# Placing sixteen gate tiles differently over the heads of a hybrid mLSTM and GLA layer

## The chip, the cores and the metric

The kernel runs on one core of a Trainium2 chip. The time is that of one execution on the device in microseconds (us), and the median of several runs is compared. Engines are named as the profile names them: PE does the matmuls (PEld its weight loads), DVE and ACT are the vector and the scalar engine, POOL is GpSimd, SP issues DMAs. L618 means line 618 of the kernel.

## The reference, cut to what matters

One layer works on 1024 latent tokens of width 1024 and a prefix of 256 context tokens. Its mixer projects the modulated input `u` with one wide matrix and feeds two recurrent branches, each run forwards and backwards, the context first:

```python
p = u @ w_in + b_in
q_m, k_m, v_m, o_m, g_m, q_g, k_g, v_g, z_g, r_g, gate_a, gate_b = jnp.split(p, cuts, axis=-1)
...
hm_c, hm_l = bidirectional(mlstm_scan, m_sh_c, m_g_c, m_sh_l, m_g_l, m_init)   # 8 heads of 128
hg_c, hg_l = bidirectional(gla_scan, g_sh_c, g_g_c, g_sh_l, g_g_l, g_init)     # 4 heads, keys 128, values 256
...
y_m = (head_norm(h_m, mlstm_norm_g, True) * sigmoid(o_m)) @ w_branch_mlstm
y_g = (head_norm(h_g, gla_norm_g, False) * silu(z_g)) @ w_branch_gla
mix = (sigmoid(gate_a) * y_m + sigmoid(gate_b) * y_g) @ w_out
```

A gated convolutional feed-forward block (ConvGLU) and two layer norms follow. The two pre-activations `gate_a` and `gate_b`, 1024 columns each, are needed only after both branches; they depend on nothing but `u`.

## The kernel before

**Matmuls.** Every product with a weight is made of three float32r matmuls (`mm3`, L279): high part by high part (L283), high by low (L284), low by high (L285). The high part of a weight block is copied out by ACT (L252, tile `whi`), the low part is the difference taken by DVE (L253, `wlo`); the raw block comes by a DMA on SP's queue. One projection of 128 columns by 512 tokens is 24 matmuls, each 128x128 by 128x512.

**Gate tiles.** `gate_a` and `gate_b` are computed in 16 gate tiles (`gate_tile`, L532) of 128 columns by 1024 tokens: two weight loads, two L252, two L253, 48 matmuls, two copies by ACT out of PSUM (L537), two DMAs issued by ACT (L538) to DRAM (`tha`, `thb`). `fill(n)` makes the next n of them; they are work for PE that no scan waits for. The loops over the heads say beside which head they are written down.

**Order.** The program is written in order of the loops, and the tile scheduler of the language then puts each engine's instructions into a fixed order of its own, by what is ready and by the order written. So a gate tile written behind a scan is spread into that scan's gaps on PE and behind it. The orders shown below are the scheduler's.

**GLA heads** (loop L862, h = 0 to 3). `gla_qk` and `gla_v` project, `log_gates` (L414: L423 on PE, L425, L428, L429 on ACT, L426, L430 on DVE, a DMA to `la`) makes the decay; head 0 does it for heads 1 to 3 as well. `gla_scan` (L571) loads the decay (L576) and exponentiates it (L577 on ACT), multiplies (L578), makes the diagonal (L596 on PE into the PSUM tag `pa`, L597 on DVE), and then runs seven levels, each of 16 matmuls (L618, into `pa`), two masked copies (L619, DVE), and three multiplications for either direction (L624, L626, L628; DVE, and on every second level POOL for one direction). Level l+1's L618 needs level l's L626, and L626 needs that level's L618 to have read `qq`. A tail (L639 to L692) follows. `late()` runs what a scan left over (its `finish`).

**The mLSTM's gates** (`ml_gates`, L439) run once between the two loops: a serial chain on DVE, four scans along the tokens among it (L456, L457, L461, L462). Around it lie the first v projection (`ml_proj_v(0)`; DVE copies its PSUM out at L713) and the first q and k projection (`ml_proj_qk`, L717).

**mLSTM heads** (loop L877, h = 0 to 7). Each pass projects q and k of the next head, every second pass v of the next pair, and writes down the scan of this head (`ml_scan`, L752). The scan's decay tiles come by POOL's DMA queue: L760 writes a mask, L761 adds a row to it, L764 loads another row; ACT exponentiates them (L765 once and L769 eight times for either direction), POOL multiplies (L766). PE then transposes k into the PSUM tag `pt` (L777), makes scores in `pa` (L786) and runs the state products (L796) and the outputs (L816, L817, into `po`). The transposes of the result (L844, into `pt`) and the copies of them by ACT (L845) belong to `finish`, which runs before the next scan. Tags of PSUM have two buffers each, so a third tile of tag `pt` waits until the first has been copied out.

Behind the loops come the z projection (`gated`, L918), the branch products, the output product and the feed-forward block; none of it is touched.

Of the kernel before, what the change touches and what calls it, by code (L numbers as in the profile page):

```python
# [24 lines left out]
MH = 8  # L25
# [11 lines left out]
def layer_kernel(ctx, tc, I, out, dbg=None):  # L37
# [16 lines left out]
    def nm(s):  # L54
        cnt[0] += 1
        return f"{s}_{cnt[0]}"
# [20 lines left out]
    def ubt(i, shape, dt=F32):  # L77
        return ub.tile(shape, dt, tag=f"u{i}", name=nm(f"u{i}"))
# [35 lines left out]
    for l in range(7):  # L114
        h = 1 << l
# [91 lines left out]
    for i in range(2):  # L207
        hi = stg.tile([P, 2, 256], F32R, tag="whi", name=nm("whi"), bufs=6)
        lo = stg.tile([P, 2, 256], F32R, tag="wlo", name=nm("wlo"), bufs=6)
        h, l = (t[:].rearrange("p a (b c) -> p (a b) c", c=P) for t in (hi, lo))  # L210
# [203 lines left out]
    def log_gates(h):  # L414

        for parts in (((0, 0), (0, 1)), ((1, 0), (1, 1)), ((0, 2), (1, 2))):
            t = slot(12 + zz[0] % 2, [P, SEQ])
            m = slot((14, 5)[zz[0] % 2], [P, SEQ])
            zz[0] += 1
            n = BW[parts[0][1]]  # L420
            for i, (d, b) in enumerate(parts):
                p = pt(("pa", "po", "pt")[(2 * zz[0] + i) % 3], [P, 512])
                T.matmul(p[:, 0:n], gws[d][:, h * P:(h + 1) * P], gr[0:96, b * 512:b * 512 + n], start=True, stop=True)  # L423
                bias = cB((c_gwf if d == 0 else c_gwb) + h)
                A.activation(t[:, i * n:i * n + n], p[:, 0:n], AF.Abs, bias=bias)  # L425
                V.tensor_scalar(m[:, i * n:i * n + n], p[:, 0:n], bias, 0.0, op0=ALU.add, op1=ALU.min)  # L426
            t, m = t[:, 0:2 * n], m[:, 0:2 * n]
            A.activation(t, t, AF.Exp, scale=-1.0)  # L428
            A.activation(t, t, AF.Ln, bias=ones[:])  # L429
            V.tensor_tensor(m, m, t, op=ALU.subtract)  # L430
            if n == 512:
                SY.dma_start(la_d[parts[0][0]][h][:, 0:SEQ], m)
            else:
                for d in range(2):
                    SY.dma_start(la_d[d][h][:, SEQ:L], m[:, d * n:d * n + n])
# [96 lines left out]
    def gate_tile(dst, off, cb0, j, tags=("pj", "pj")):  # L532
        w = wtile(w_in, off + j * P)
        for b in range(2):
            p = proj(w, 0, b, tags[b])
            t = sc.tile([P, 512], F32, tag="gt", name=nm("gt"), bufs=2)
            A.activation(t[:], p[:], AF.Identity, scale=0.5, bias=cB(cb0 + j))  # L537
            A.dma_start(dst[j][:, b * 512:b * 512 + 512], t[:])  # L538

    def gla_qk(h):  # L540
        w = wload([(w_in, O_QG + h * P, P, 0), (w_in, O_KG + h * P, P, P)], eng=V)
        q = slot(0, [P, SEQ])
        k = slot(1, [P, L])
        for b in range(2):
            p = proj(w, 0, b)
            A.activation(q[:, b * 512:b * 512 + 512], p[:], AF.Identity, scale=QS, bias=cB(c_qg + h))
        for b in range(3):
            p = proj(w, P, b)
            A.activation(k[:, b * 512:b * 512 + BW[b]], p[:, 0:BW[b]], AF.Identity, bias=cB(c_kg + h))
        return q, k  # L550

    def gla_v(h):
        vb = vbias(O_VG + h * 256)
        w = wload([(w_in, O_VG + h * 256, 256, 0)], eng=V)
        vs = [slot(2 + 2 * (h % 2) + i, [P, 5, 256]) for i in range(2)]
        for t0 in range(0, 10, 2):
            p = pt("pj", [P, 2, 256])
            for i in range(2):
                mm3(p[:, i, :], u_tok(t0 + i), lambda k: w(k, 0, 256))
            if t0 < 8:  # L560
                V.tensor_tensor(vs[t0 // 4][:, t0 % 4:t0 % 4 + 2, :], p[:],
                                vb[:].unsqueeze(1).to_broadcast([P, 2, 256]), op=ALU.add)
            else:
                for i in range(2):
                    V.tensor_tensor(vs[i][:, 4, :], p[:, i, :], vb[:], op=ALU.add)

        def v(c):
            return vs[c // 4][:, c % 4, :] if c < 8 else vs[c - 8][:, 4, :]
        return v
# [132 lines left out]
    def ml_proj_v(pr):  # L702
        w = wload([(w_in, O_VM + pr * 256, 256, 0)], eng=V)
        vb = vbias(O_VM + pr * 256)
        vs = [slot(2 + i, [P, 10, 129]) for i in range(2)]
        for t in vs:
            G.memset(t[:, :, 128:129], 1.0)
        for t0 in range(0, 10, 2):
            p = pt("pj", [P, 2, 256])
            for i in range(2):  # L710
                mm3(p[:, i, :], u_tok(t0 + i), lambda k: w(k, 0, 256))
            for e in range(2):
                V.tensor_tensor(vs[e][:, t0:t0 + 2, 0:P], p[:, :, e * P:(e + 1) * P],  # L713
                                vb[:, e * P:(e + 1) * P].unsqueeze(1).to_broadcast([P, 2, P]), op=ALU.add)
        return vs

    def ml_proj_qk(h):  # L717
        w = wload([(w_in, O_QM + h * P, P, 0), (w_in, O_KM + h * P, P, P)])
        res = []
        for i in range(2):  # L720
            n = SEQ if i == 0 else L
            y = slot((0, 4)[h % 2] + i, [P, n])
            t0, t1, t2 = (cB(c_cv + 16 * j + 8 * i + h) for j in range(3))
            bs, b0, b2 = (cvb[:, j, 8 * i + h:8 * i + h + 1] for j in range(3))

            def tap(o, src, t):
                V.scalar_tensor_tensor(y[:, o:o + src.shape[1]], src, t, y[:, o:o + src.shape[1]],
                                       op0=ALU.mult, op1=ALU.add)
            for b in range(2 + i):
                m, o = BW[b], b * 512  # L730
                p = proj(w, i * P, b, ("pj", "pa")[(i + b) % 2])
                A.activation(y[:, o:o + m], p[:, 0:m], AF.Identity, scale=t1, bias=bs)
                tap(o + 1, p[:, 0:m - 1], t0)
                tap(o, p[:, 1:m], t2)
                if b == 0:
                    ed = sc.tile([P, 1], F32, tag="ed", name=nm("ed"), bufs=2)
                    V.tensor_copy(ed[:], p[:, m - 1:m])  # L737
                if b == 1:
                    tap(o, ed[:], t0)
                    tap(o - 1, p[:, 0:1], t2)  # L740

                if b != 1:
                    V.tensor_tensor(y[:, o:o + 1], y[:, o:o + 1], b0, op=ALU.subtract)
                if b != 0:
                    V.tensor_tensor(y[:, o + m - 1:o + m], y[:, o + m - 1:o + m], b2, op=ALU.subtract)
            th = slot(15, [P, n])
            A.activation(th[:], y[:], AF.Tanh, scale=1.0 / QS if i == 0 else 1.0)
            V.scalar_tensor_tensor(y[:], th[:], 1.0, y[:], op0=ALU.add, op1=ALU.mult)
            res.append(y)
        return res  # L750
# [101 lines left out]
    def late():  # L852
        while rest:
            rest.pop()()
# [3 lines left out]
    def fill(n, tags=("pj", "pj")):  # L858
        for _ in range(n):
            gate_tile(*gates.pop(0), tags)  # L860

    for h in range(GH):  # L862
        q, k = gla_qk(h) if h else (q0, k0)
        v = gla_v(h)
        late()
        if h == 0:
            for i in range(1, GH):
                log_gates(i)
            fill(1)
        rest.append(gla_scan(h, q, k, v))  # L870
        if h:
            fill(1)
    v2 = ml_proj_v(0)
    qk = ml_proj_qk(0)
    late()
# [1 line left out]
    for h in range(MH):  # L877
        nxt = ml_proj_qk(h + 1) if h + 1 < MH else None
        if h and h % 2 == 0:
            v2 = ml_proj_v(h // 2)  # L880
        if h == MH - 1:
            fill(1, ("pj", "pa"))
        late()
        rest.append(ml_scan(h, *qk, v2[h % 2]))
        qk = nxt
        fill(2 if h < 2 or h == 6 else 1, ("pj", "pa"))
    while gates:
        fill(1)

# [362 lines left out]
    for j, c in enumerate(todo[len(main):]):  # L1252
        if j >= 6:
            if j < 10:
                h = (ubt(10 + j - 6, [P, 2, 512], F32R) if j < 8 else
                     fin.tile([P, 2, 512], F32R, tag="gl", name=nm("wlate"), bufs=2))
                h = [h[:, 0, :], h[:, 1, :]]
            else:
                h = [fin.tile([P, 512], F32R, tag="z1", name=nm("wlate"), bufs=4)[:] for _ in range(2)]
# [40 lines left out]
```

## Time and profile before

| | |
|---|---|
| median of 3 runs | 2279.73 us (2279.18 to 2281.49) |
| the profiled execution | 2277.97 us |
| its span, from the first to the last instruction | 2276.2 us |
| mean granted PE clock over the span | 0.997 of full speed |
| PE busy | 2229.1 us, 98% of the span |
| DVE, ACT, POOL busy | 1322.5, 728.4, 253.3 us |
| chain of work that ended last | PE 86%, DVE 6%, DMA 5% |

PE is busy nearly always, so a change of order can only take from or add to the some 47 us in which it is not, or to the clock at which it works. The span is read stretch by stretch: GLA head 0 lies around 137 to 178 us, head 3 up to 500, the mLSTM's gates at 500 to 560, the mLSTM's heads from there to 1100.

### The profile page before, as it was taken

How to read it: one execution, taken by the hardware profiler on the slowest of the kernel's cores; microseconds unless marked ns; L12 is line 12 of the kernel's file. 1: busy time of each engine (PE TensorE's matmuls, PEld its weight loads, DVE VectorE, ACT ScalarE, POOL GpSimd, SP SyncE). 2: the span in 40 equal slices, each digit the busy share in tenths (PEclk: the TensorE clock that was granted, in tenths of full speed). 3: DMA queues.
4: the chain of work that ended last, by engine and by line, in shares of the span. 5: the costliest groups of instructions: out<-in, count | busy, mean ns of one | idle time of the engine just before them, and what ended most of it. 6: DMA issues, size and time to landing. Idle time of an engine off the chain costs nothing.

```text
span 2276.2 us, 30329 instructions
## 1 busy us (share of the span) xinstructions
PE 2229.1 (98%) x11641; PEld 1876.1 (82%) x11641; DVE 1322.5 (58%) x2511; ACT 728.4 (32%) x1239; POOL 253.3 (11%) x254
## 2 busy tenths in 40 slices
PE   8989999999999999999999999999999999999998
PEld 4979898988889889898887788787888888888886
DVE  6485737377664655755356433578765655654257
ACT  3562323233333332313431333313333333333110
POOL 1010101021110111101210122102101000000100
PEclk9999999999999999999999999999999999999999
DMA  8231221203432433324358544515311222235722
GB/s 289 68 120 52 61 63 38 70 31 99 107 103 65 114 98 103 102 79 126 93 181 269 182 125 139 198 48 173 96 56 38 67 76 72 75 105 177 226 75 74
DMA packets 187746, 246.55 MB, mean 108 GB/s; under 512 B 16257, under 2 KB 129537, under 8 KB 187601
## 3 DMA queue, kind: packets, MB, share of 16 engines
q1 hardware_dynamic: 164673, 179.16, 25.2%
q0 software_dynamic: 12416, 44.21, 7.4%
q10 hardware_dynamic: 10512, 21.24, 2.5%
q8 instruction: 91, 1.49, 0.3%
q14 instruction: 54, 0.44, 0.1%
HBM read 186.57 MB, written 49.60 MB: 104 GB/s over the span
## 4 chain that ended last, share of the span: by engine, by line
PE 86%; DVE 6%; DMA 5%; ACT 1%; issue 1%; POOL 0%; SPq 0%; DVEq 0%; ACTq 0%; POOLq 0%
PE pj L285 16%; PE pj L283 16%; PE pj L284 16%; PE pa L283 4%; PE pa L284 4%; PE pa L285 4%; DMA u<-in_w_mod_dram 2%; PE pa L618 2%; PE pt L796 1%; PE po L816 1%; PE po L817 1%; PE po L284 1%; PE po L285 1%; PE po L283 1%; PE pt L659 1%
## 5 line engine op out<-in xcount | busy, mean ns | idle before, releaser
L253 DVE TENSOR_TENSOR wlo<-raw,whi 128x512 fp32r<-128x512 f32 x302 | 217.8, 725 | 161.7 <-ACT whi L252 158.1
L283 PE MATMUL pj<-s,whi 128*128 128x512 f32 x784 | 305.9, 391 | 0.4 <-ACT val L1123 0.4
L285 PE MATMUL pj<-s,wlo 128*128 128x512 f32 x784 | 306.0, 390 | 0.0
L252 ACT ACTIVATE whi<-raw 128x512 fp32r<-128x512 f32 x302 | 188.4, 629 | 334.9 <-PE pj L285 152.0
L284 PE MATMUL pj<-s,whi 128*128 128x512 f32 x744 | 290.7, 391 | 2.9 <-POOL s L1091 2.8
L1147 DVE SCALAR_TENSOR_TENSOR acc<-g,colF,acc 128x945 f32<-128x945 f32 (+2 forms) x168 | 206.2, 1228 | 139.9 <-ACT acc L1138 137.8
L283 PE MATMUL pj<-u,whi 128*128 128x512 f32 (+1 forms) x528 | 206.2, 391 | 4.0 <-ACT whi L252 4.0
L285 PE MATMUL pj<-u,wlo 128*128 128x512 f32 (+1 forms) x528 | 205.8, 390 | 0.9 <-DVE wlo L253 0.9
L284 PE MATMUL pj<-u,whi 128*128 128x512 f32 (+1 forms) x528 | 205.4, 389 | 0.0
L283 PE MATMUL pj<-whi,u 128*128 128x256 f32 x640 | 181.8, 284 | 0.0
L285 PE MATMUL pj<-whi,u 128*128 128x256 f32 x640 | 181.7, 284 | 0.0
L284 PE MATMUL pj<-wlo,u 128*128 128x256 f32 x640 | 181.7, 284 | 0.0
L283 PEld LDWEIGHTS pj<-s,whi 128*128 128x128 f32 x784 | 147.3, 188 | 33.2 <-issue 1.7
L285 PEld LDWEIGHTS pj<-s,wlo 128*128 128x128 f32 x784 | 147.3, 188 | 31.2 <-DVE wlo L253 0.5
L284 PEld LDWEIGHTS pj<-s,whi 128*128 128x128 f32 x744 | 139.8, 188 | 34.3 <-POOL s L1091 4.1
L283 PE MATMUL pa<-u,whi 128*128 128x512 f32 (+1 forms) x376 | 141.6, 376 | 1.1 <-DVE ed L737 1.1
L284 PE MATMUL pa<-u,whi 128*128 128x512 f32 (+1 forms) x376 | 141.3, 376 | 0.0
L285 PE MATMUL pa<-u,wlo 128*128 128x512 f32 (+1 forms) x376 | 140.8, 374 | 0.0
L284 PEld LDWEIGHTS pj<-wlo,u 128*128 128x128 f32 x640 | 123.0, 192 | 0.0
L283 PEld LDWEIGHTS pj<-whi,u 128*128 128x128 f32 x640 | 123.0, 192 | 0.1
L285 PEld LDWEIGHTS pj<-whi,u 128*128 128x128 f32 x640 | 123.0, 192 | 0.0
L283 PEld LDWEIGHTS pj<-u,whi 128*128 128x128 f32 x528 | 99.6, 189 | 22.9 <-ACT whi L252 4.4
(500 smaller groups left out, 4353.9 us busy)
## 6 DMA issues: line engine op xcount, KB each, us to landing
u<-in_w_mod_dram SPq DMA_DIRECT2D x48, 512.0 KB
raw<-in_w_in_dram SPq DMA_DIRECT2D x96, 256.0 KB
raw<-in_w_up_dram SPq DMA_DIRECT2D x176, 128.0 KB
raw<-in_w_in_dram SPq DMA_DIRECT2D x96, 128.0 KB
raw<-in_w_down_dram SPq DMA_DIRECT2D x44, 256.0 KB
qq<-re POOLq DMA_DIRECT2D x16, 512.0 KB, 5.7
s<-rmask POOLq DMA_DIRECT2D x16, 512.0 KB, 5.2
s<-rr POOLq DMA_DIRECT2D x16, 512.0 KB, 8.5
```

The lines of the kernel that those rows point to most:

```text
L252: A.activation(hi, src, AF.Copy)
L253: eng.tensor_tensor(lo, src, hi.bitcast(F32), op=ALU.subtract)
L283: T.matmul(p, lh, rh, start=k == 0, stop=False)
L284: T.matmul(p, lh, rl, start=False, stop=False)
L285: T.matmul(p, ll, rh, start=False, stop=k == nk - 1)
L618: T.matmul(p[:, c, :], kc[:, o:o + P], pairs(qq, 1, hs, o, 64 // hs), start=True, stop=True)
L659: T.matmul(p[:], t[:, c * P:(c + 1) * P], v(c), start=True, stop=True)
L796: T.matmul(p[:, i, :], kt[d][:, c, :], v[:, c, :], start=True, stop=True)
L816: T.matmul(p[:, i, :], dt_[d][:, c, :], v[:, c, :], start=True, stop=False)
L817: T.matmul(p[:, i, :], et[d][:, c * P:(c + 1) * P], cs[d][:, c, :], start=False, stop=True)
L1147: V.scalar_tensor_tensor(av, g[:, r0 + dy:r1 + dy, c0 + dx:c1 + dx], convw(3 * ky + kx, f), av, op0=ALU.mult, op1=ALU.add)
```

## The change

```diff
@@ GLA loop
         if h == 0:
             for i in range(1, GH):
                 log_gates(i)
-            fill(1)
+            fill(2)
         rest.append(gla_scan(h, q, k, v))
         if h:
-            fill(1)
+            fill(2)
     v2 = ml_proj_v(0)
@@ mLSTM loop
         rest.append(ml_scan(h, *qk, v2[h % 2]))
         qk = nxt
-        fill(2 if h < 2 or h == 6 else 1, ("pj", "pa"))
+        fill(1 if h + 1 < MH else 0, ("pj", "pa"))
     while gates:
         fill(1)
```

All 16 gate tiles are made in both versions. Before, the GLA heads have one each and the mLSTM heads 2, 2, 1, 1, 1, 1, 2 and, for the last, one ahead of its scan (`if h == MH - 1: fill(1)`, unchanged) and one behind it. Afterwards the GLA heads have two each, the mLSTM heads 0 to 6 one each, and the last only the one ahead of its scan.

**PE around scan 7.** The last head's scan on PE, before: the rows from the end of the gate tiles on. Between the last L817 of scan 6 and the first of these L844 stand 110 matmuls of the projections and gate tiles. `pa_9442` is a gate tile's PSUM tile, `pt_9471` and `pt_9477` hold head 6's transposed result.

```order
L284 MATMUL pa_9442<-u_61_314,whi_9410 128x512
L285 MATMUL pa_9442<-u_53_306,wlo_9411 128x512
L844 MATMUL pt_9471<-ident,s_1270_9154 128x128 [waits DVE_49] x4
L844 MATMUL pt_9477<-ident,s_1270_9154 128x128 [waits DVE_49] x4
L786 MATMUL pa_9535<-s_1219_8586,s_1224_8652 128x128 [waits Activation_49]
L786 MATMUL pa_9535<-s_1219_8586,s_1224_8652 128x128 x3
L777 MATMUL pt_9516<-ident,s_1224_8652 128x128 [waits Activation_49]
```

The same place afterwards (other numbers, the same tiles): between scan 6's last L817 and this L844 stand 62 matmuls.

```order
L284 MATMUL pa_9510<-u_61_314,whi_9478 128x512
L285 MATMUL pa_9510<-u_53_306,wlo_9479 128x512
L844 MATMUL pt_9539<-ident,s_1290_9290 128x128 [waits DVE_49] x4
L844 MATMUL pt_9545<-ident,s_1290_9290 128x128 [waits DVE_49] x4
L786 MATMUL pa_9603<-s_1239_8722,s_1244_8788 128x128 [waits Activation_49]
L786 MATMUL pa_9603<-s_1239_8722,s_1244_8788 128x128 x3
L777 MATMUL pt_9584<-ident,s_1244_8788 128x128 [waits Activation_49]
```

The order of the scan is the same; one gate tile of 48 matmuls is gone from in front of it.

**ACT at the same place.** Before, from the exponentials of scan 7's decay (L769) to the copies of head 6's result (L845):

```order
L769 ACTIVATE s_1323_9501<-s_1323_9501,ta 128x128 x6
L252 ACTIVATE whi_9782<-raw_9780 128x512 [waits PE_49]
L252 ACTIVATE whi_9788<-raw_9786 128x512 [waits DMAHW4_49,PE_49]
L537 ACTIVATE gt_9399<-pa_9374,colB 128x512 [waits DMAHW0_49,PE_49]
L538 DMA tha_863<-gt_9399 128x512 [waits Activation_49]
L537 ACTIVATE gt_9439<-pj_9414,colB 128x512 [waits DMAHW2_49,PE_49]
L538 DMA tha_864<-gt_9439 128x512 [waits Activation_49]
L252 ACTIVATE whi_9794<-raw_9792 128x512 [waits DMAHW7_49,PE_49]
L252 ACTIVATE whi_9800<-raw_9798 128x512 [waits DMAHW1_49,PE_49]
L537 ACTIVATE gt_9467<-pa_9442,colB 128x512 [waits DMAHW4_49,PE_49]
L845 ACTIVATE s_1316_9470<-pt_9471,colB 128x512 [waits DMAHW3_49,PE_49]
```

And afterwards:

```order
L769 ACTIVATE s_1333_9569<-s_1333_9569,ta 128x128 x6
L252 ACTIVATE whi_9959<-raw_9957 128x512 [waits DMAHW4_49,PE_49]
L252 ACTIVATE whi_9965<-raw_9963 128x512 [waits DMAHW5_49,PE_49]
L537 ACTIVATE gt_9535<-pa_9510,colB 128x512 [waits DMAHW0_49,PE_49]
L845 ACTIVATE s_1326_9538<-pt_9539,colB 128x512 [waits DMAHW3_49,PE_49]
```

In both orders L845 stands behind all of scan 7's exponentials, two weight copies and an L537; six rows that lay between are gone.

**PE in GLA head 0.** Between two levels of the scan, before (`pa_1405` to `pa_1432` are the levels' PSUM tiles, `pj_1779` is part of head 1's q and k projection); nine to eleven such matmuls stand behind most levels:

```order
L618 MATMUL pa_1411<-qq_1352,s_218_1402 128x128 x3
L284 MATMUL pj_1779<-u_57_310,whi_1707 128x512
L285 MATMUL pj_1779<-u_49_302,wlo_1708 128x512
L283 MATMUL pj_1779<-u_50_303,whi_1714 128x512
L284 MATMUL pj_1779<-u_58_311,whi_1714 128x512
L285 MATMUL pj_1779<-u_50_303,wlo_1715 128x512
L283 MATMUL pj_1779<-u_51_304,whi_1714 128x512
L284 MATMUL pj_1779<-u_59_312,whi_1714 128x512
L285 MATMUL pj_1779<-u_51_304,wlo_1715 128x512
L283 MATMUL pj_1779<-u_52_305,whi_1721 128x512
L618 MATMUL pa_1426<-qq_1352,s_221_1423 128x128 [waits DVE_49,Activation_49,Pool_49]
```

Afterwards levels 1 to 4 stand behind one another with nothing between; these are the rows from level 1's second half on:

```order
L618 MATMUL pa_1479<-qq_1420,s_228_1470 128x128 x3
L618 MATMUL pa_1494<-qq_1420,s_231_1491 128x128 [waits DVE_49,Activation_49,Pool_49]
L618 MATMUL pa_1494<-qq_1420,s_231_1491 128x128 x3
L618 MATMUL pa_1500<-qq_1420,s_231_1491 128x128 [waits PE_49]
L618 MATMUL pa_1500<-qq_1420,s_231_1491 128x128 x3
L618 MATMUL pa_1515<-qq_1420,s_234_1512 128x128 [waits DVE_49,PE_49,Activation_49]
L618 MATMUL pa_1515<-qq_1420,s_234_1512 128x128 x3
L618 MATMUL pa_1521<-qq_1420,s_234_1512 128x128 [waits PE_49]
```

The second gate tile of head 0 stands ahead of the scan's first matmuls (L596), and head 1's projection, which stood between the levels, is mostly used up by then.

## Rows read from the trace of the kernel before

**Rows 1.** Page, part 1: span, and busy time of each engine.

```profile
span 2276.2 us, 30329 instructions
PE 2229.1 (98%) x11641; PEld 1876.1 (82%) x11641; DVE 1322.5 (58%) x2511; ACT 728.4 (32%) x1239; POOL 253.3 (11%) x254
```

**Rows 2.** Waits of PE: total us, times, longest us.

```profile
PE pa L618 <- DVE qq L626: 8.4, 13, 1.7
PE pa L596 <- DVE s L426: 4.7, 1, 4.7
PE pj L283 <- ACT whi L252: 4.0, 1, 4.0
```

**Rows 3.** Timeline of PE, GLA head 0: start, duration, [idle before <- releaser].

```profile
137.91 1.05 PE L596 MATMUL pa<-s,s 128*128 128x128 f32 x8
145.01 2.07 PE L596 MATMUL pa<-s,s 128*128 128x128 f32 x8 [4.67 <-DVE s L426]
147.62 3.10 PE L618 MATMUL pa<-qq,s 128*128 128x128 f32 x16
...
158.76 2.02 PE L618 MATMUL pa<-qq,s 128*128 128x128 f32 x16 [1.68 <-DVE qq L626]
...
175.66 2.02 PE L618 MATMUL pa<-qq,s 128*128 128x128 f32 x16 [0.31 <-DVE qq L626]
```

**Rows 4.** Busy time in stretches of head 0, PEclk the granted clock.

```profile
142.50:145.00 2.50, 0.00 (x0) 0.00 (x0) 2.50 (x5) 2.47 (x5) 0.00 (x0) 0.96 0.00 0
145.00:147.50 2.50, 2.49 (x11) 2.31 (x11) 2.50 (x6) 1.51 (x4) 0.00 (x0) 0.50 0.65 256
147.50:150.00 2.50, 2.50 (x15) 2.38 (x14) 2.36 (x4) 2.50 (x6) 0.00 (x0) 0.86 0.61 162
```

**Rows 5.** The same view where L283 waits for `whi`.

```profile
1262.50:1265.00 2.50, 0.14 (x1) 0.00 (x0) 1.53 (x3) 0.00 (x0) 0.00 (x0) 1.00 0.95 294
...
1267.50:1270.00 2.50, 2.50 (x7) 1.99 (x8) 2.13 (x4) 0.00 (x0) 0.00 (x0) 0.56 0.94 289
1270.00:1272.50 2.50, 2.50 (x8) 1.28 (x7) 0.62 (x1) 0.63 (x1) 0.00 (x0) 0.76 0.85 281
```

**Rows 6.** Timeline of PE, GLA head 3, first, third and last of six waits.

```profile
451.75 2.92 PE L618 MATMUL pa<-qq,s 128*128 128x128 f32 x16 [0.74 <-ACT s L612]
...
467.10 2.02 PE L618 MATMUL pa<-qq,s 128*128 128x128 f32 x16 [1.28 <-DVE qq L626]
...
479.88 2.02 PE L618 MATMUL pa<-qq,s 128*128 128x128 f32 x16 [0.30 <-DVE gdec L632]
```

**Rows 7.** Timeline of PE, GLA head 1, last of three waits.

```profile
253.19 2.02 PE L618 MATMUL pa<-qq,s 128*128 128x128 f32 x16 [1.14 <-DVE qq L626]
```

**Rows 8.** Busy time, sum of eight windows from 520 to 560 us.

```profile
sum 40.00, PE 36.82 PEld 30.48 DVE 31.53 ACT 18.39 POOL 6.77; mean PE 4.60 PEld 3.81 DVE 3.94 ACT 2.30 POOL 0.85
```

**Rows 9.** Timeline of PE from the first fill behind scan 6 to scan 7.

```profile
1022.48 0.48 PE L284 MATMUL pa<-u,whi 128*128 128x512 f32 x1
...
1047.53 1.04 PE L844 MATMUL pt<-ident,s 128*128 128x128 f32 x8
...
1049.34 0.44 PE L777 MATMUL pt<-ident,s 128*128 128x128 f32 x2
```

**Rows 10.** Timeline of ACT at the same place.

```profile
1035.48 2.45 ACT L769 ACTIVATE s<-s,ta 128x128 f32<-128x128 f32 x8 [3.31 <-DMA s<-rr]
...
1041.93 1.14 ACT L252 ACTIVATE whi<-raw 128x512 fp32r<-128x512 f32 x2
1042.97 0.67 ACT L537 ACTIVATE gt<-pa,colB 128x512 f32<-128x512 f32 x1
...
1048.61 0.68 ACT L845 ACTIVATE s<-pt,colB 128x512 f32<-128x512 f32 x1
```

**Rows 11.** Timelines of DVE and PE behind scan 7: normalisation of head 7, its transposes.

```profile
1076.20 2.14 DVE L837 TENSOR_SCALAR s<-s,mst,mrs 128x128 f32<-128x128 f32 x8
1095.77 1.03 PE L844 MATMUL pt<-ident,s 128*128 128x128 f32 x8
```

## The prediction

> **What bounds the kernel now.** I read the page's first part before anything else: PE is busy for 2229.1 of 2276.2 us and no other engine for more than 58% [rows 1]. Moving 16 gate tiles about leaves PE's work the same, so the time can change only where PE stands still, 47.1 us in all, or where its clock falls. So I went next to PE's waits: the largest are L618 on DVE's L626 (8.4 us in 13 pieces, the GLA levels), L596 on L426 (4.7 us at once, GLA head 0), and L283 on `whi` (4.0 us at once, near 1263 us) [rows 2]. The last belongs to the stretch behind the loops, whose order the change leaves alone; it is of use only as a price. Third, the timelines and windows of the stretches to which gate tiles come or from which they go. A gate tile is a reserve of PE work that waits for no scan. It is worth something only where a scan's chain on other engines is longer than the PE work that lies ready, and costs something where it is taken from such a place. So each stretch has one question: what is the chain, and how much work is left to lay over it.
>
> **Two prices used throughout.** The 110 matmuls from 1022.48 to 1047.53 start 0.2277 us apart [rows 9], so a gate tile's 48 are 10.93 us. And the price of a clock that fell: after the wait of 4.67 us in head 0, during which PE did nothing for a whole window while DVE was fully busy [rows 4], the granted clock is 0.50 (the 1.2 GHz level) from 145 to 147.5 us, 0.86 to 150. The same eight L596 take 2.07 us there and 1.05 us before it, the 16 L618 take 3.10 us against 2.02 on later levels [rows 3]: 1.02 + 1.08 = 2.1 us. After the 4.0 us near 1263 the clock is 0.56 and then 0.76 [rows 2, 5]. After waits of 1.68 us and less L618 keeps its 2.02 us [rows 3, 6, 7]. The Trainium skill ("TensorE: Matmul & The Clock Gate", Terms) prices a throttled stretch at its length times one half; by that rule the two windows of rows 5 cost some 1.7 us in place of 2.1 (an estimate); by it each fall below would cost 0.4 us less.
>
> **The change, stretch by stretch.**
>
> GLA head 0 (137 to 178 us). The second gate tile now lies ahead of L596, so the 4.67 us of idle there [rows 3] is covered. But L596 waits for DVE's log-gate work, DVE is fully busy through it [rows 4], and no PE work makes DVE faster. I followed the new order with the durations of the old trace: the first level starts at about 147.5 us as before. What covered that wait is missing between the levels: levels 1 to 4 have no matmul between them now. Their pace is the chain L618, L626, L618, which takes 28.0 us for six steps (147.62 to 175.66) [rows 3]; 9 to 11 matmuls per gap were 2.0 to 2.5 us of that. In the walk PE then waits about 4.3, 3.0 and 2.2 us ahead of levels 2, 3 and 4. Both accounts nearly cancel: the last level starts about 0.2 to 0.3 us earlier, but PE has done about 0.85 us less of its other work, a loss of 0.6 us if the clock stays up. It probably falls once, since 4.3 us lies between the 4.0 and 4.7 us after which it fell, and not near the 1.68 us after which it did not; that is 2.1 us. I take +2.7. Bounds: ACT's log-gate work ends some 3 us earlier in the new order (L577, which waited for a DMA in front of it, is behind it now), which would be a gain of about 3 if DVE could follow; and the clock low through all four levels is a loss up to 8 (rival below).
>
> GLA heads 1 and 2. PE's order within the scan keeps the same number of matmuls in each gap, 7 to 11. Their waits (three, the last of 1.14 us [rows 7], in sum 2.16) stay: 0.
>
> GLA head 3. The six waits from 0.74 to 0.30 us sum to 3.94 us [rows 6]. The order becomes that of heads 1 and 2, whose waits sum to 2.16: a gain of 1.7 or 1.8; I take 1.7, bounds 0 and 3.9.
>
> The mLSTM's gates (520 to 560 us). PE is busy 36.82 of 40 us, so 3.2 us are lost to DVE's serial scans [rows 8]. There are 10.93 us of PE work more around it, but the copies L713 stand between those scans on DVE, and the projections on PE wait for them; in the walk 1.4 us remain. Gain 1.8, bounds 0 and 3.2.
>
> mLSTM heads 0 to 6. Between the scans of head 0 and head 1 there are still 120 matmuls, 27.3 us, and elsewhere no fewer. A scan's preparation takes about 20 us from the end of the scan before it (1022.48 to 1043.1, [rows 9, 10]). Covered: 0.
>
> **Scan 6 to scan 7, the term that decides.** Before, the 110 matmuls cover 25 us here, and at their pace without a gap, PE has no idle time [rows 9]. The cover shrinks to 62 matmuls, 14.1 us, because head 6 gives up one gate tile ahead of scan 7. PE's order at this place is L844 (result of head 6 into both `pt` buffers), half of L786, then L777, which needs a `pt` buffer that ACT's L845 has to empty. Before, L777 starts at 1049.34 us, right behind the first L845 (1048.61 + 0.68) [rows 9, 10]; that L845 waited for PE. With one gate tile less in front L777 could start at 1049.34 − 10.93 = 1038.4. But L845 stands on ACT behind scan 7's exponentials, two L252 and one L537, and these don't move with PE: the first L769 waits until 1035.48 for POOL's DMA of `rr`, which adds onto a mask written into the buffer that scan 6's last L816 still reads: its start hangs on scan 6's end. From there ACT is busy without a gap through L769, L765 and L252 (1041.93 + 1.14) and an L537 (0.67) to 1043.6 [rows 10]. L845 follows at 0.68: L777 at 1044.3, 5.9 us after it could. Nothing else is ready for PE: what stands behind L777 in its order is the scan itself (L816, L796 need it), and the z projection behind that. An idle stretch of 5.9 us is longer than the two after which the clock fell, so I add one fall, 2.0 us. Loss 7.9. Bounds: if the DMAs land 2 us earlier since less weight traffic is under way, 3.9 and a fall that costs nothing; if they land 1 us later and the clock costs 2.1 to 3, up to 9.9. Behind scan 7 59 matmuls lie ahead of its own L844 in place of 110, which brings it forward by 11.6 us, from 1095.77 to 1084.2; DVE's normalisation, which it waits for, ends at 1078.3 [rows 11], so nothing is added.
>
> **The sum.** +2.7 − 1.7 − 1.8 + 7.9 = +7.1 us, on the profiled execution 2277.97 + 7.1 = 2285.1. The profiled execution lies 1.76 below the median of the runs shown, so on the median 2279.73 + 7.1 = 2286.8. A difference of 0.2%, 4.6 us, is about what a measurement of this kernel can tell from none.
>
> **Rivals.**
>
> The clock stays low in head 0 (chance 0.17). With waits of 4.3, 3.0 and 2.2 us and only 2 us of matmuls between them, PE might not get its clock back before level 5. The 16 L618 then take 3.1 us and more in place of 2.02 on four levels, and they are on the levels' chain: 4.3 to 8 us in place of 2.1. Total +9.3 to +13, about 2291. The Trainium skill's clock page (HAM oscillation) describes just such a loop, in which every short burst between waits starts cold; in [rows 4] the clock was back at 0.86 in the second window, but that was with fill between the levels, so no row here shows the loop.
>
> Scan 7's stall is mostly hidden and the falls of the clock don't come (0.22). The decay DMAs, issued while the same queue carries less, land earlier, and ACT reaches L845 near 1040. Then the loss there is 2 to 4 us, head 0 costs 0.6, and −3.5 is earned: −1 to +1, about 2280, no measurable change. For it: the 3.31 us wait on `rr` is the longest piece of the ACT chain and a DMA's. Against it: its start hangs on scan 6's end and not on the fill.
>
> Faster (0.06). One mechanism: DVE in head 0. If the log gates, ready on ACT some 3 us earlier, let DVE start the levels 3 us earlier, the whole head ends that much earlier and head 0 is −2.4 in place of +2.7. Alone it gives +2; it decides only if scan 7's loss is under 0 as well, that is if L845 is free before 1038.4, with which the sum is −5.9, about 2274. Against it: DVE has no gap to give up from 142.5 to 147.5 us [rows 4].
>
> The change does nothing (0.05): PE's total is equal and every wait just changes place, 2279.7. The forecast itself has 0.50.
>
> **How the numbers follow.** The likeliest gives 2286.8. The range takes the hidden stall at its low end and the low clock at its high end: 2280 to 2293. Slower by over 0.2% means above 2284.3: the forecast holds four fifths of it beyond that bound, and the low-clock rival all of it plus little else, 0.50 x 0.85 + 0.17 + 0.06 of the hidden case = 0.66. Faster means below 2275.2: 0.06. Same: 0.28.
>
> **What would show it.** Of the changed kernel's PE timeline: L596 of head 0 without a wait, levels 2 to 4 each with a wait of 2 to 5 us on L626, the clock below 1 in a window of 155 to 170 us; the six waits of head 3 near 2.2 us in sum; windows around the gates' scans with about 1.4 us idle; and one wait of L777 on L845 of about 6 us at some 1045 us, followed by a window with a clock near 0.5. Without that wait the prediction is wrong in its main term; if ACT's L769 starts earlier against scan 6's end than 13 us (1035.48 − 1022.48), the DMA step failed; if it is there and the time hardly moved, the gains of the GLA heads were underrated.

## The result

The changed kernel takes 2293.04 us (median of 6 runs, 2291.82 to 2295.74) against 2280.14 us for the kernel before in the same comparison: the ratio is 1.0058, with a 95% interval from 1.0048 to 1.0069. It is 12.9 us slower; 7.1 were forecast, and the range ended at 2293. The profiled execution took 2295.74 us, the slowest of the six. Its page, part 1 (compare [rows 1]):

```profile
span 2294.0 us, 30334 instructions
PE 2237.0 (98%) x11641; PEld 1881.2 (82%) x11641; DVE 1319.9 (58%) x2511; ACT 728.6 (32%) x1239; POOL 254.2 (11%) x254
```

The number of matmuls is the same, but PE is busy 7.9 us longer with them, so part of the loss is a lower clock (mean granted clock 0.992 over the span, before 0.997); in the other 9.9 us of the longer span PE is idle. Its waits (total us, times, longest; compare [rows 2]):

```profile
PE pa L618 <- DVE qq L626: 13.1, 12, 3.8
PE pt L777 <- ACT s L845: 5.9, 1, 5.9
PE pj L283 <- ACT whi L252: 5.1, 1, 5.1
PE pa L618 <- ACT s L612: 3.7, 3, 1.4
...
PE pa L786 <- DVE s L727: 1.2, 1, 1.2
...
PE pa L596 <- DVE s L426: 0.3, 1, 0.3
```

The wait of L596 is down to 0.3 us from 4.7, as the change would have it. The waits of the GLA levels on L626 are 4.7 us longer in sum, and L777 waits 5.9 us for L845, which it did not do before. The timeline of PE shows the places (compare [rows 3, 9]):

```profile
143.62 1.16 PE L596 MATMUL pa<-s,s 128*128 128x128 f32 x8 [0.32 <-DVE s L426]
147.43 2.92 PE L618 MATMUL pa<-qq,s 128*128 128x128 f32 x16
...
152.43 2.16 PE L618 MATMUL pa<-qq,s 128*128 128x128 f32 x16 [1.65 <-DVE qq L626]
158.34 3.75 PE L618 MATMUL pa<-qq,s 128*128 128x128 f32 x16 [3.75 <-DVE qq L626]
164.18 3.42 PE L618 MATMUL pa<-qq,s 128*128 128x128 f32 x16 [2.09 <-DVE qq L626]
169.53 2.84 PE L618 MATMUL pa<-qq,s 128*128 128x128 f32 x16 [1.92 <-DVE s L628]
175.99 1.95 PE L618 MATMUL pa<-qq,s 128*128 128x128 f32 x16
180.09 2.02 PE L618 MATMUL pa<-qq,s 128*128 128x128 f32 x16
...
373.64 3.23 PE L618 MATMUL pa<-qq,s 128*128 128x128 f32 x16 [1.32 <-ACT s L612]
...
1066.87 1.03 PE L844 MATMUL pt<-ident,s 128*128 128x128 f32 x8
...
1074.66 0.69 PE L777 MATMUL pt<-ident,s 128*128 128x128 f32 x2 [5.86 <-ACT s L845]
```

The seven levels of head 0 (0 to 6) are the rows from 147.43 to 180.09. They start at the old time, but the last one starts 4.4 us later: from the first to it 32.7 us pass (147.43 to 180.09) in place of 28.0, and levels 2 to 4 take 3.75, 3.42 and 2.84 us in place of 2.02. The windows of the same execution give the granted clock (the column behind POOL's, compare [rows 4]):

```profile
157.50:160.00 2.50, 1.66 (x8) 1.69 (x9) 2.13 (x4) 0.63 (x1) 0.21 (x2) 0.50 0.00 0
160.00:162.50 2.50, 2.10 (x10) 1.80 (x9) 1.67 (x3) 0.31 (x1) 1.95 (x2) 0.50 0.01 3
162.50:165.00 2.50, 0.82 (x4) 0.85 (x5) 2.50 (x6) 0.84 (x2) 0.00 (x0) 0.50 0.00 0
...
375.00:377.50 2.50, 2.50 (x12) 2.33 (x11) 1.44 (x3) 0.62 (x2) 2.19 (x2) 0.57 0.01 3
...
1072.50:1075.00 2.50, 0.34 (x2) 0.34 (x3) 1.89 (x3) 2.50 (x5) 0.61 (x1) 0.50 0.13 14
1075.00:1077.50 2.50, 2.50 (x14) 2.50 (x13) 1.35 (x3) 0.18 (x1) 0.00 (x0) 0.50 0.97 306
```

Head 0 runs at the 1.2 GHz level through its levels 2 and 3, and scan 7 starts at that level too. Why L777 waits stands in ACT's timeline (compare [rows 10]; its first row belongs to GLA head 1 and is used below):

```profile
253.68 1.21 ACT L612 ACTIVATE s<-kk 128x512 f32<-128x512 f32 x2 [3.68 <-DMA hg<-s]
...
1065.25 2.45 ACT L769 ACTIVATE s<-s,ta 128x128 f32<-128x128 f32 x8 [2.62 <-DMA s<-rr]
...
1072.33 1.13 ACT L252 ACTIVATE whi<-raw 128x512 fp32r<-128x512 f32 x2
1073.37 0.67 ACT L537 ACTIVATE gt<-pa,colB 128x512 f32<-128x512 f32 x1
1073.94 0.67 ACT L845 ACTIVATE s<-pt,colB 128x512 f32<-128x512 f32 x1
```

PE has both transposes done by 1067.9, and ACT is busy from 1065.25 on with the exponentials, the weight copies and an L537, one behind the other, before it comes to L845.

**An account by places.** To compare two orders of the same matmuls, take one instruction that stands in both, the difference of its start times, and subtract the 128x512 matmuls that the new order has placed ahead of it in addition, at 0.2277 us each [rows 9]. What is left is time lost up to there. Start times are from the two traces, the counts of matmuls from the two orders; the last column is the same for a second profiled execution of the changed kernel (the run e11 below).

| first matmul of | before, us | changed, us | matmuls more ahead | lost up to there | second execution |
|---|---|---|---|---|---|
| L596, GLA head 1 | 229.75 | 245.95 | 48 | 5.3 | 5.6 |
| L596, GLA head 3 | 443.40 | 484.72 | 144 | 8.5 | 9.3 |
| L777, mLSTM head 0 | 583.77 | 633.37 | 192 | 5.9 | 6.4 |
| L777, mLSTM head 1 | 646.67 | 685.36 | 144 | 5.9 | 6.4 |
| L777, mLSTM head 2 | 737.41 | 766.65 | 96 | 7.4 | 7.9 |
| L777, mLSTM head 6 | 1000.53 | 1029.82 | 96 | 7.4 | 8.0 |
| L844 ahead of scan 7 | 1047.53 | 1066.87 | 48 | 8.4 | 8.9 |
| L777, mLSTM head 7 | 1049.34 | 1074.66 | 48 | 14.4 | 14.9 |
| L844 behind head 7 | 1095.77 | 1112.06 | 0 | 16.3 | 16.8 |
| end of the span | 2276.2 | 2294.0 | 0 | 17.8 | 16.2 |

So: 5.3 us lost in GLA head 0, 3.2 in heads 1 and 2, 2.6 gained in head 3 and the gates' stretch, 1.5 lost in the scan of mLSTM head 1, nothing more up to head 6, 8.9 around scan 7 (1.0 of it in scan 6, where L817 waits 0.67 us for DVE's L806, and 7.9 from the L844 ahead of scan 7 to the one behind it), and 1.5 behind the loops, which the second execution does not have.

### The profile page after: what moved, and what is told of

It is laid out like the page before. It is cut to its first block, busy times and chain, and to the rows that moved or that the text cites. A ratio compares the mean times of both kernels' runs of the same rounds, so it can differ in the third digit from the quotient of the medians.

```text
span 2294.0 us, 30334 instructions
## 1 busy us (share of the span) xinstructions
PE 2237.0 (98%) x11641; PEld 1881.2 (82%) x11641; DVE 1319.9 (58%) x2511; ACT 728.6 (32%) x1239; POOL 254.2 (11%) x254
## 4 chain that ended last, share of the span: by engine, by line
PE 89%; DVE 5%; DMA 4%; ACT 1%; issue 1%; POOL 0%; SPq 0%; DVEq 0%; ACTq 0%; POOLq 0%
PE pj L283 16%; PE pj L285 16%; PE pj L284 16%; PE pa L283 4%; PE pa L284 4%; PE pa L285 4%; PE pa L618 2%; PE po L283 2%; PE po L284 2%; PE po L285 2%; PE po L816 1%; PE pt L796 1%; PE po L817 1%; DMA u<-in_w_mod_dram 1%; PE pt L659 1%; PE pj L1190 1%
## 5 line engine op out<-in xcount | busy, mean ns | idle before, releaser
L283 PE MATMUL pj<-s,whi 128*128 128x512 f32 x784 | 305.6, 390 | 0.1
L283 PE MATMUL pj<-u,whi 128*128 128x512 f32 (+1 forms) x560 | 219.9, 393 | 5.6 <-ACT whi L252 5.1
L285 PE MATMUL pj<-u,wlo 128*128 128x512 f32 (+1 forms) x560 | 219.0, 391 | 0.0
L284 PE MATMUL pj<-u,whi 128*128 128x512 f32 (+1 forms) x560 | 218.7, 390 | 0.0
L283 PE MATMUL pj<-whi,u 128*128 128x256 f32 x640 | 181.3, 283 | 0.6 <-DVE s L713 0.6
L283 PEld LDWEIGHTS pj<-s,whi 128*128 128x128 f32 x784 | 147.1, 188 | 33.2 <-issue 1.7
L283 PE MATMUL pa<-u,whi 128*128 128x512 f32 (+1 forms) x344 | 129.1, 375 | 0.0
L284 PE MATMUL pa<-u,whi 128*128 128x512 f32 (+1 forms) x344 | 129.0, 375 | 0.0
L285 PE MATMUL pa<-u,wlo 128*128 128x512 f32 (+1 forms) x344 | 128.6, 374 | 0.0
L283 PEld LDWEIGHTS pj<-u,whi 128*128 128x128 f32 x560 | 106.3, 190 | 26.1 <-ACT whi L252 5.5
L283 PEld LDWEIGHTS pj<-whi,u 128*128 128x128 f32 x640 | 122.8, 192 | 0.9 <-PE pj L285 0.7
```

The lines of the kernel that those rows point to most:

```text
L283: T.matmul(p, lh, rh, start=k == 0, stop=False)
L284: T.matmul(p, lh, rl, start=False, stop=False)
L285: T.matmul(p, ll, rh, start=False, stop=k == nk - 1)
```

## The experiments

Times are medians; the kernel before was run on the same chip each time (2280.81 us with the first four, 2281.2 with the next four, 2281.38 with the last). Edits are shown against the changed kernel, that of e6 against the kernel before. The theory: the losses are local, one where head 0's gaps were emptied and one where scan 7 lost its cover, and L845's place on ACT's queue makes the second.

**e1: scan 7's cover back, taken from GLA head 3.**

```diff
         if h:
-            fill(2)
+            fill(2 if h < 3 else 1)
...
-        fill(1 if h + 1 < MH else 0, ("pj", "pa"))
+        fill(2 if h == 6 else 1 if h + 1 < MH else 0, ("pj", "pa"))
```

> Head 6 of the mLSTM has its second gate tile again; GLA head 3 gives it up (tiles 2, 2, 2, 1 and 1 x 6, 2, 1). Theory (each loss is local): scan 7 has its 110 matmuls of cover again, the wait of L777 on L845 (5.9 us) and the low clock behind it are gone, about 8 to 9 us less than the changed kernel, minus 1 to 2 us that the gates' stretch no longer gains: about 2286. Rival (the loss at scan 7 is made up or passed on behind it, at the wait on the weights near 1284 us): under 4 us less, 2289 or more.

2291.31 us, ratio 1.0044 (1.0031 to 1.0057). Scan 7 has no wait and by the account loses nothing from head 6's L777 (12.7 us lost up to there) to the L844 behind head 7 (12.75). But the gates' stretch, without head 3's second tile, loses 0.8 us (8.85 to 9.7) where the change gained 2.6, and 3.1 more are lost by mLSTM head 2. In time it is the rival's number, by the account the theory's: taking the tile from head 3 cost 3.4 us in the gates' stretch and 1.6 more in the first mLSTM heads, over half of what scan 7 gained.

**e2: both places back.** Here the tile for head 6 comes from GLA head 0.

```diff
                 log_gates(i)
-            fill(2)
+            fill(1)
...
-        fill(1 if h + 1 < MH else 0, ("pj", "pa"))
+        fill(2 if h == 6 else 1 if h + 1 < MH else 0, ("pj", "pa"))
```

> Head 6 has its second gate tile again and GLA head 0 only one ahead of its scan (tiles 1, 2, 2, 2 and 1 x 6, 2, 1). Theory (two local losses, head 0 and scan 7): both gone, 5 us at head 0 and 8 to 9 at scan 7, so 2279 to 2281, no different from before. Rival (the losses share a cause, such as the granted clock, and don't add up): at least 3 us above the sum, 2283 or more.

2280.83 us, ratio 0.9997 (0.9989 to 1.0006): the whole loss of the change is gone with these two places.

**e3: head 0 back alone.** As e2, but with `fill(1, ...)` behind every mLSTM head, the last one too.

> Only GLA head 0 gives a gate tile back, which goes behind the last mLSTM scan (tiles 1, 2, 2, 2 and 1 x 7, 1 + 1). Theory (head 0 pays for emptied gaps between its levels): about 5 us less than the changed kernel, 2287 to 2288, with the wait of L777 on L845 still 6 us long. Rival (the whole of head 0's loss is chance of the clock in the profiled execution): 2291 to 2293.

2288.65 us, ratio 1.0032 (1.0020 to 1.0045): 4.4 us less than the change. L777 still waits:

```profile
1056.88 0.69 PE L777 MATMUL pt<-ident,s 128*128 128x128 f32 x2 [6.14 <-ACT s L845]
```

e2 and e3 differ by one gate tile, ahead of scan 7 or behind it: 7.8 us. That is the price of scan 7's cover, in time.

**e4: the changed kernel with head 6's result copied first.** `late()` runs before the last gate tile, which puts L845 ahead of most of scan 7's exponentials on ACT.

```diff
+        late()
         if h == MH - 1:
             fill(1, ("pj", "pa"))
-        late()
```

> The changed kernel's tiles, but head 6's result is transposed and copied ahead of the last gate tile, so that ACT's L845 stands in front of most of scan 7's exponentials. Theory (L777 waits only because L845 is late in ACT's queue): the wait of 5.9 us and the fall of the clock behind it go, 6 to 8 us less than the changed kernel, 2285 to 2287, with 14 us of cover as in the changed kernel. Rival (14 us of cover are too few for the scan's decay tiles themselves): L816 waits for the exponentials instead, and the time falls by under 3 us, 2290 or more.

2291.91 us (2288.91 to 2293.59), ratio 1.0049 (1.0035 to 1.0063): in time the rival's number. L777 no longer waits for L845, the clock stays up at this place, and by the account the stretch from head 6's L777 to the L844 behind head 7 loses 3.8 us in place of 8.9; but PE waits 2.09 us for an L537, and the median is only 1.1 us lower than the change's, less than its runs scatter. How much L845's place is worth can't be told from this; e8 asks it again without head 0's second tile.

**e8: e3 with head 6's result copied first** (the edits of e3 and e4).

> GLA head 0 with one tile (tiles 1, 2, 2, 2 and 1 x 7, 1 + 1, as in the run that gave back head 0's tile alone) and head 6's result transposed and copied ahead of the last gate tile: L845's place alone, without head 0's scatter. Theory (the loss at scan 7 is L845's place in ACT's queue): 4 to 5 us less than that run's 2288.65, 2283 to 2285. Rival (14 us of cover are too few in any order, the wait goes to L537 and the exponentials): 2287 to 2289.

2286.05 us (2283.08 to 2289.71, 11 runs), ratio 1.0022 (1.0013 to 1.0031): 2.6 us less than e3, between the theory and the rival. In PE's timeline the wait has changed its cause:

```profile
1055.15 1.16 PE L786 MATMUL pa<-s,s 128*128 128x128 f32 x8 [2.43 <-ACT gt L537]
```

The second half of L786 needs a `pa` buffer, which the last gate tile holds until ACT has come past the exponentials to its L537. So L845's place was a part of the loss: some third of the 7.8 us in time, and by the account 4.5 us of e3's 8.0 in the profiled execution, which is the fastest of the eleven. Behind it stands the next copy in the same queue, and 62 matmuls don't cover scan 7 in this order either.

**e12: e8 once more,** for its profiled execution.

> The run with head 0's tile back and head 6's result copied ahead of the last gate tile, once more, since its profiled execution was the fastest of eleven. If the wait at scan 7 hangs on when the decay DMAs land, this execution has a longer one (over 3 us in place of 2.4) where it is slower than 2285; if scan 7 repeats within 0.5 us, the scatter is elsewhere.

2280.80 us, with a wait on L537 of 1.80 us and 2.8 us lost around scan 7, against 2.43 and 3.5 in e8's. Of e8's eleven times the lowest is 2283.08. The scatter of this kernel is larger than this difference; where it comes from stays open.

**e5: head 0's second tile behind its scan.**

```diff
                 log_gates(i)
-            fill(2)
+            fill(1)
         rest.append(gla_scan(h, q, k, v))
-        if h:
-            fill(2)
+        fill(2 if h else 1)
```

> The changed kernel's tiles, but the second one of GLA head 0 is written behind its scan in place of ahead of it; the scheduler then puts 8, 0, 11, 1, 11 and 10 matmuls between the levels in place of 0, 0, 0, 0, 13 and 9. Theory (head 0 pays for gaps with nothing in them, and the place ahead of the scan is the cause): two thirds of head 0's 5 us come back, 2289 to 2290. Rival (a second tile in head 0 costs wherever it stands): 2292 to 2294.

2292.00 us (2287.42 to 2293.71), ratio 1.0039 (1.0025 to 1.0052). In its profiled execution head 0 loses 0.7 us and the clock does not fall there; L777's wait is 6.25 us and scan 7 costs 10.5 in place of 8.9. In time only 1 us came back, which is the rival's number; scan 7 hides a part of the rest. The pair e9 and e10 takes scan 7 out.

**e9 and e10: the same question with scan 7 covered.** Both give head 6 its second tile, taken from GLA head 1. e9 has head 0's second tile behind the scan, e10 ahead of it.

```diff
@@ e9 @@
                 log_gates(i)
-            fill(2)
+            fill(1)
         rest.append(gla_scan(h, q, k, v))
-        if h:
-            fill(2)
+        fill(1 if h < 2 else 2)
@@ e10 @@
         if h:
-            fill(2)
+            fill(1 if h == 1 else 2)
@@ both @@
-        fill(1 if h + 1 < MH else 0, ("pj", "pa"))
+        fill(2 if h == 6 else 1 if h + 1 < MH else 0, ("pj", "pa"))
```

> GLA head 0 with one gate tile ahead of its scan and one behind it, head 6 of the mLSTM with its second tile again, taken from GLA head 1 (tiles 1 + 1, 1, 2, 2 and 1 x 6, 2, 1). Scan 7 is covered as before the change, so that head 0 stands alone. Theory (the place ahead of the scan is what costs, since it leaves the gaps between the levels empty): 2281 to 2283, within 2 us of the kernel before. Rival (a second tile in head 0 costs wherever it stands): 2285 to 2287, the same as the next run.

> As the run before it, but both tiles of GLA head 0 stand ahead of its scan, as in the change (tiles 2, 1, 2, 2 and 1 x 6, 2, 1). Theory (empty gaps between levels 1 to 4 and the clock that falls in them): 4 to 6 us more than the run before it, 2286 to 2288. Rival (head 0's loss in the profiled execution is not typical): within 1.5 us of the run before it.

e9: 2279.36 us, ratio 0.9992 (0.9984 to 1.0001). e10: 2287.30 us, ratio 1.0026 (1.0017 to 1.0036). The place of that one tile is worth 7.9 us. Between the levels from the first on stand 8, 0, 11, 1, 11 and 10 matmuls in e9, and 0, 0, 0, 0, 13 and 9 in e10. Timeline of PE in e9, levels 2 to 4 of head 0:

```profile
158.21 3.27 PE L618 MATMUL pa<-qq,s 128*128 128x128 f32 x16 [2.41 <-DVE qq L626]
164.23 1.95 PE L618 MATMUL pa<-qq,s 128*128 128x128 f32 x16
168.10 2.02 PE L618 MATMUL pa<-qq,s 128*128 128x128 f32 x16 [1.70 <-DVE qq L626]
```

And in e10:

```profile
158.30 2.74 PE L618 MATMUL pa<-qq,s 128*128 128x128 f32 x16 [2.36 <-DVE qq L626]
163.55 3.75 PE L618 MATMUL pa<-qq,s 128*128 128x128 f32 x16 [2.51 <-DVE qq L626]
169.22 3.75 PE L618 MATMUL pa<-qq,s 128*128 128x128 f32 x16 [1.93 <-DVE s L628]
```

Up to head 1's L596 e9 has lost 0.35 us and e10 5.2; the rest of the difference arises in heads 1 and 2, where e10 loses 3.1 more, with the clock at 0.50 in head 2 (365 to 367.5 us), and e9 nothing.

**e7: matmuls that nobody needs, in head 0's empty gaps.**

```diff
                 V.copy_predicated(am[:, 4 * g:4 * g + 4, :], lmask[:, l, :].unsqueeze(1).to_broadcast([P, 4, P]), p[:])
+            if h == 0 and 1 <= l <= 4:
+                p = pt("po", [P, 4, P])
+                for c in range(12):
+                    T.matmul(p[:, c % 4, :], kc[:, 0:P], q[:, 0:P], start=True, stop=True)
```

> The changed kernel with 48 matmuls of 128x128 more in GLA head 0, 12 to each of the levels 1 to 4, on inputs that are there, into an unused PSUM tile; nothing reads them, the output is that of the reference. Theory (most of head 0's loss is the clock that falls when PE waits between the empty levels): L618 takes 2.0 us on all levels again, 2 to 4 us less than the changed kernel although PE does more, 2289 to 2291. Rival (the loss is the waits on DVE themselves, work not done): the added 5 us of matmuls lie in the waits and gain nothing, or cost up to 3: 2293 to 2296.

2296.21 us, ratio 1.0062 (1.0049 to 1.0074): no faster than the change, the rival's number. The pace of the levels did come back; timeline of PE (L630 here is L626 of the others), then a window:

```profile
159.83 2.05 PE L618 MATMUL pa<-qq,s 128*128 128x128 f32 x16 [0.38 <-POOL qq L630]
165.13 2.02 PE L618 MATMUL pa<-qq,s 128*128 128x128 f32 x16 [0.55 <-DVE qq L630]
169.41 2.02 PE L618 MATMUL pa<-qq,s 128*128 128x128 f32 x16
```

```profile
160.00:165.00 5.00, 4.58 (x38) 4.22 (x38) 5.00 (x9) 1.89 (x3) 1.92 (x2) 1.00 0.01 2
```

With PE busy the clock is 1.00 throughout, L618 takes 2.02 us, and from the first level to the last 28.9 us pass (149.22 to 178.10) in place of 32.7. But the scheduler placed 14 fewer useful matmuls ahead of the last level, and the first level started 1.8 us later. So with PE kept busy the levels are 3.8 us shorter, and the time is lost all the same if what fills the gaps is not work that has to be done: by the account head 0 loses 6.7 us here, and heads 1 and 2, in both of which the clock fell in this execution (0.57 from 257.5 and 0.50 from 377.5 us), 4.3. The theory's time was missed.

**e6: the kernel before, with the tile behind the last scan moved to GLA head 3.**

```diff
         if h:
-            fill(1)
+            fill(2 if h == 3 else 1)
...
-        fill(2 if h < 2 or h == 6 else 1, ("pj", "pa"))
+        fill(2 if h < 2 or h == 6 else 1 if h + 1 < MH else 0, ("pj", "pa"))
```

> The kernel before with one move only: the gate tile behind the last mLSTM scan goes to GLA head 3 (tiles 1, 1, 1, 2 and 2, 2, 1, 1, 1, 1, 2, 1). Theory (the one part of the change that gains: head 3 and the gates' stretch have 3 to 4 us of idle PE to cover, and the place behind the last scan needs no cover): 2 to 3 us less than the kernel before, about 2278. Rival (the gates' stretch gives it back at the first mLSTM heads, or behind the loops): 2280 to 2282.

2279.01 us (11 runs) against 2281.2 (21 runs), ratio 0.9987 (0.9979 to 0.9996): faster than the kernel before by 2.2 us. By the account it has gained 2.5 us when mLSTM head 0 begins, and keeps 2.3 to the L844 behind head 7; behind the loops, in code that is the same, the profiled execution then loses 3.5 us against that of the kernel before, which was a fast one (2277.97 us, 3.2 below the median here). In the gates' stretch PE waits only twice in the timeline:

```profile
531.65 0.36 PE L283 MATMUL pj<-whi,u 128*128 128x256 f32 x1 [0.56 <-DVE s L713]
538.08 0.47 PE L283 MATMUL pj<-u,whi 128*128 128x512 f32 x1 [0.45 <-DVE s L713]
```

**e11: the changed kernel once more.**

> The changed kernel once more, for a second profiled execution. If the first one was typical, the account by stretches repeats within 1 us: 5 us at head 0, 3 in heads 1 and 2, 2.6 back at head 3 and the gates, 9 at scan 7. If the granted clock falls at different places from one execution to the next, terms of head 0 and of heads 1 and 2 differ by 1 to 3 us while the wait of L777 on L845 stays between 5 and 7 us.

2294.53 us (4 runs), ratio 1.0059 (1.0043 to 1.0074). The account is in the table above: head 0, the gates and scan 7 repeat within 0.4 us, L777's wait is 5.86 us again, heads 1 and 2 cost 3.6 in place of 3.2.

## Why the prediction was wrong, step by step

- **Scan 7, the term of 7.9 us: right, in place and size.** The wait of L777 on L845 was forecast at 5.9 us and is 5.86 in two executions, and L769 starts 12.6 us behind scan 6's end (1052.67 to 1065.25) for 13.0. With the clock's fall, 1.9 us, the stretch from one L844 to the next costs 7.9 us in both executions by the account, and 7.8 by e3 against e2. The other 1.0 us of the 8.9 is lost in scan 6 and was not forecast. That nothing is added behind scan 7 held too: L844 there waits for nothing.
- **GLA head 0, the term of 2.7: wrong in size, and this is the main step that failed.** The places were right (first level at 147.43 for 147.5; waits ahead of levels 2 to 4 of 3.75, 2.09 and 1.92 us for 4.3, 3.0 and 2.2). The step "It probably falls once ... that is 2.1 us" was not: the clock stayed at its lower level through levels 2 and 3 and partly 4, and the three L618 alone took 1.7 + 1.4 + 0.8 = 3.9 us more. The term is 5.3 and 5.6 us, and 7.9 by e9 against e10 with what follows in heads 1 and 2. The price of one fall was misread as well: the first level's 16 L618 take 2.92 us at the full clock too (451.75 in [rows 6], 147.43 above; granted clock 1.00 at both), so of the 3.10 in [rows 3] only 0.18 belongs to the clock, and that fall cost 1.2 us, not 2.1. This was the rival "The clock stays low in head 0", priced 4.3 to 8 us and given a chance of 0.17. The cause given for it stands: e10 and e9 differ only in where one tile stands, and so in how many of the gaps are empty.
- **GLA heads 1 and 2, taken as 0: lost 3.2 us, and 3.6 in the second execution.** The matmuls in their gaps are as many as before, as was said; but the wait ahead of their first level grew from 0.54 to 1.41 us in head 1. ACT's L612 there waits for the DMA that stores the head before's result, whose buffer the copy reuses. Before, ACT waited 2.79 us for it:

```profile
236.59 1.26 ACT L612 ACTIVATE s<-kk 128x512 f32<-128x512 f32 x2 [2.79 <-DMA hg<-s]
```

  and afterwards 3.68 (above). The wait goes with the second tile: in head 1 it is 2.79 to 3.53 us in the four profiled executions with one tile there and 3.55 to 4.33 in the ten with two. That the tile's transfers make that DMA slower is likely, but was not tested. In head 2 the clock fell behind this wait (0.57 at 375 us), and the first level took 3.23 us, against 2.92 in head 1 of the same execution, with the five matmuls behind it slower too. Where head 0 has one tile and heads 1 and 2 still have two (e2, e3, e8, e12), these heads lose 1.3 to 1.6 us by the account, so about half of the 3.2 goes with head 0's tile.
- **GLA head 3 and the gates, 1.7 + 1.8 gained: right in place, somewhat too large.** 2.6 and 2.9 us by the account, and e6, which makes this move alone, is 2.2 us faster in time. PE's waits went from 3.94 to 2.94 us in head 3 (2.2 were forecast) and from 3.2 to 1.0 in the gates' stretch (1.4 were forecast).
- **mLSTM heads 0 to 6, "Covered: 0": wrong by 1.5 us** in the scan of head 1, where L786 has a new wait on DVE's L727. PE's row, then ACT's ahead of it:

```profile
688.13 0.71 PE L786 MATMUL pa<-s,s 128*128 128x128 f32 x4 [1.21 <-DVE s L727]
```

```profile
668.29 1.06 ACT L765 ACTIVATE qq<-qq 128x1024 f32<-128x1024 f32 x1 [9.03 <-DMA qq<-re]
669.26 0.76 ACT L732 ACTIVATE s<-pj,cvb,colB 128x512 f32<-128x512 f32 x1
670.74 4.39 ACT L769 ACTIVATE s<-s,ta 128x128 f32<-128x128 f32 x14 [0.72 <-DMA s<-rr]
```

  L786 needs a `pa` buffer, which the last block of head 2's projection holds until DVE has added its taps (L727). The taps follow ACT's copies L732, and these stand between scan 1's exponentials (L765, L769), which wait for their DMAs. The 120 matmuls were compared with the exponentials alone, and the chain goes on from them over L732 and L727 to PE. That this order on ACT makes the taps late is read from one trace and was not tested. From head 2's L777 to head 6's the 0 held.
- **The sum.** 7.1 was forecast; by the account 5.3 + 3.2 − 2.6 + 1.5 + 8.9 + 1.5 = 17.8 in the first profiled execution and 16.2 in the second, 12.9 in the medians. The two executions profiled stand 2.7 us above and 0.4 below their medians, and that of the kernel before 2.2 below its own; so the account's places and order are shown, its last 1 to 2 us are not.

## What to carry to other kernels

Count the independent matmuls that lie over every wait for another engine before moving one, and compare them with the longest chain of all that end there, not with the chain that comes to mind first: here a tile of 10.9 us taken from ahead of scan 7 cost 7.8, and the second tiles of GLA heads 1 and 2, whose waits were 2.5 and 2.3 us in sum before, gained nothing. Filler belongs where the waits are. In the GLA scan they lie between the levels, so a tile written behind the scan's start was worth 7.9 us more (e9 against e10) than one ahead of it, which uses up at once the work that would have filled the gaps; at scan 7 the wait lies ahead of the scan, and so must the tile. A PE that idled between short bursts lost twice here, by the waits and by its clock, and the lower clock lengthened the very chain for which it waited: 32.7 us for the levels of head 0, 28.9 with PE kept busy.

## What the hardware showed unexpectedly

The length of a single wait did not tell whether the clock would fall. Before the change it fell after waits of 4.7 and 4.0 us and not after 1.68 [rows 2 to 5]. In e5 and e9 level 2 of head 0 stands behind the same wait of 2.41 us; in e9 the clock fell there (0.75 and then 0.57 in the windows from 157.5 to 162.5 us; its 16 L618 take 3.27 us, row above), in e5 it did not (1.00 in both windows):

```profile
159.01 2.02 PE L618 MATMUL pa<-qq,s 128*128 128x128 f32 x16 [2.41 <-DVE qq L626]
```

In the changed kernel it fell in GLA head 2 behind a wait of 1.32 us (0.57 of full speed at 375 us). In the second execution (e11) the clock is 1.00 there, behind a wait of 1.39, and fell in head 1 instead, behind one of 2.01; two windows of it:

```profile
257.50:260.00 2.50, 2.50 (x12) 2.40 (x11) 1.21 (x2) 0.40 (x1) 2.19 (x2) 0.52 0.00 0
...
375.00:377.50 2.50, 2.07 (x12) 2.07 (x13) 2.28 (x4) 1.68 (x3) 0.48 (x1) 1.00 0.00 0
```

Between two bursts of L618 the lower level could hold over several waits: 0.50 from 157.5 to 165 us, although PE worked 4.6 of those 7.5 us. The Trainium skill ("TensorE: Matmul & The Clock Gate", HAM oscillation) describes a loop whose every burst starts cold behind a wait; head 0 of the change is such a place, with 3.75, 3.42 and 2.84 us for a burst of 2.02. The waits that the Trainium skill gives for its loop are 3 to 5 us; those here are 1.9 to 3.75.
